# Two-layer decoder trunk: the four-expert round in fourth place, the rare-overflow branch and the overflow fetch behind round three, parameter rows behind the 37th expert unit

## The chip, the cores and the metric

The kernel runs on one NeuronCore of a Trainium2 chip. The metric is the device time of one execution in microseconds (us). The engines are named as in the profile: PE (TensorE, matrix multiplications; PEld is its weight load), DVE (VectorE), ACT (ScalarE), POOL (GpSimd) and SP (SyncE, which issues the transfers here); a q behind a name is the engine's sequencer, which runs branches, waits and the issue of transfers.

## The reference, cut to what matters

Two layers over 256 tokens of width 1024. Each layer is a token mixer (pooling, a gated convolution, differential attention and spatial gating, merged by gates) and then a mixture of experts; both end in a residual and a layer norm.

```python
def hierarchical_moe(x, w_rg, b_rg, w_re, b_re, w_gate, w_up, w_down):
    gl = (x @ w_rg + b_rg)                       # 4 groups
    pg = softmax(gl); g_sel = argmax(gl); p_sel = pg[g_sel]
    el = einsum('bsd,gde->bsge', x, w_re) + b_re # 4 experts in a group
    top_v, top_i = top_k(el[g_sel], 2)
    gate = softmax(top_v) * p_sel                # two experts of 16 per token
    ...
    for e in range(16):                          # width 1024 -> 256 -> 1024
        h = silu(x @ w_gate[e]) * (x @ w_up[e])
        out += gate[:, e] * (h @ w_down[e])
```

Which experts are full depends on the data. All weights have to come from memory once, since the on-chip memory holds a small part of them.

## The kernel before, in words

**Units and loads.** Weights arrive in units of 1 MB (class `Unit`, L117): one transfer each, issued by SP in the order in which the units are used. Fourteen buffers go round, so the load of unit i goes into the buffer of unit i-14 and is issued when that unit has been used. Units 0 to 47 of the expert part of a layer are three for each of 16 experts: two halves of gate and up (kh=0, kh=1) and one of down. Units 48 to 51 are the first four of the next layer, for the first layer alone.

**Rounds.** The experts run in seven rounds, p = 0 to 6, each with 128 gathered token slots. Rounds 0 to 2 take the first six experts in pairs of 64 slots. The other ten are sorted by their count of tokens: rounds 3 to 5 take the six fullest in pairs, round 6 the four emptiest at 32 slots each (`PAIRS`, `HALF`, `places`). The list `feed` gives the order of the units: for each round its gate and up units, then the down units of the round before. A four-expert round therefore has eight gate and up units and four down units, a pair four and two.

**Order of the work.** `pair(p)` writes it out by hand: `start(p+1)` (first halves of gate and up, L699), `turn(p)` (transposes on PE, L738 and L740, copied by ACT), the scatter of round p-1 into four accumulators (L715), `end(p+1)`, and `down(p)` (L707). I call the matmuls of L699 gu(round, half). `residual_mm` adds the residual in between. Behind round 5, `down7` is the second product of the last round, and its result goes through ACT and DVE (`y`, L96 and L97) into the last scatter, from which the layer norm starts. On ACT, the casts of the next layer's first units (`ahead`, L134) stand between.

**Branches.** An expert with more tokens than slots has an overflow. The usual case of one such chunk is handled in two blocks: the fetch of its three units (L797: ow twice, od; 3 MB), and its computation behind round 5 (L852). The fetch block is taken in the second layer and not in the first. Everything beyond that is in a third block, `rare` (L807), which holds further fetches and is not taken in either layer with this data. An engine that skips a block brings its semaphores to the state that they would have behind it. For SP this means eight semaphores of its transfers and one more.

**Parameter rows.** `lnp` (tile `gb2`, L815) are the scale and shift rows of the second layer norm, 1 MB. `rw` and `bc` (L1095, L1096) are small rows of the token mixer; those of the first layer are loaded at the start, those of the second during the first.

```python
        with tc.If(most > 16 * CAP + 15):          # L797
            fetch(0, ww, wd)
        ...
            si, todo = pair(NP - 4, si, todo)      # pair(3)
            residual_mm(0, hl)
            ps = start(NP - 2)                     # gu(5, 0)
        with tc.If(rest > 16 * CAP + 15, ...):     # L807
            steps.rare()
```

Of the kernel before, what the change touches and what calls it, by code (L numbers as in the profile page):

```python
# [11 lines left out]
F32 = mybir.dt.float32  # L12
# [21 lines left out]


STAT = 6
PAIRS = 6
HALF = CAP // 2
NP = PAIRS + 1
SLOTS = NP * 128  # L40
CYCLE = RAW + SPL
FIRST = CYCLE + 3
# [27 lines left out]
def trunk(ctx: ExitStack, tc: tile.TileContext, x, xT, wu, rows, brow, lnp, cst, ut, out):  # L70
# [40 lines left out]
    class Unit:  # L111


        def __init__(self, l, i, pieces=1, raw=None, src=None):
            self.raw = raw if raw is not None else raw_p.tile([P, 2048], F32, tag="raw", name=nm("raw"))
            if pieces:
                self.load = nc.sync.dma_start(self.raw, wu[l * NU + i] if src is None else src)  # L117
            self.parts = {}
            self.after = None

        def quarter(self, q):
            if q % 2 == 0:
# [294 lines left out]
    def tail(l, x_in, mhi, mlo, rw, wg, sw, unit, last):  # L417
# [15 lines left out]

        def places(p):

            w = CAP if p < PAIRS else HALF
            c, c0 = (0, p * P) if p < STAT // 2 else (1, (p - STAT // 2) * P)
            return [(2 * p + j, slice(j * w, (j + 1) * w), xg[c], slice(c0 + j * w, c0 + (j + 1) * w)) for j in range(P // w)]

        def places_n(p):  # L440
            return [2 * p + j for j in range(2 if p < PAIRS else 4)] if 0 <= p < NP else []

        feed = [f_ for p in range(NP + 1) for f_ in [(i, j) for j in range(2) for i in places_n(p)] + [(i, 2) for i in places_n(p - 1)]]
        at = {f_: i for i, f_ in enumerate(feed)}
# [104 lines left out]
        with manual():  # L549
# [66 lines left out]
                    gathered(0, k)  # L616

            key = sm.tile([P, 16], F32, tag="key", name=nm("key"))
            top = sm.tile([P, 20], F32, tag="top", name=nm("top"))
            topi = sm.tile([P, 20], I32, tag="topi", name=nm("topi"))  # L620
            ei = sm.tile([P, 20], I32, tag="ei", name=nm("ei"))

            def counts():

                V.scalar_tensor_tensor(key, cn, 16.0, down15, op0=OP.mult, op1=OP.add)
                V.max(top[:, 10:18], key[:, STAT:])
                low = sm.tile([P, 18], F32, tag="low", name=nm("low"))
                V.tensor_scalar(low[:, 0:10], key[:, STAT:], -1.0, None, op0=OP.mult)
                V.max(low[:, 10:18], low[:, 0:10])
                V.tensor_scalar(top[:, 16:20], low[:, 10:14], -1.0, None, op0=OP.mult)  # L630
                V.max(top[:, 0:8], key)
                V.scalar_tensor_tensor(top[:, 8:9], top[:, 0:1], -16.0 * MORE, top[:, 1:2], op0=OP.add, op1=OP.max)
                V.scalar_tensor_tensor(top[:, 8:9], top[:, 19:20], 16.0 * (CAP - HALF), top[:, 8:9], op0=OP.add, op1=OP.max)
# [16 lines left out]
            def slot_gates(p0, p1):  # L650
                gp = psumd()[:, :(p1 - p0) * 8].rearrange("p (a b) -> p a b", b=8)
                for p in range(p0, p1):
                    n = len(places_n(p))
                    for t in range(2):
                        T.matmul(gp[:, p - p0, :2 * n], Q[t][:, p * P:(p + 1) * P],
                                 rts[t].gh[:, 2 * p:2 * p + n, :].rearrange("p a b -> p (a b)"), start=(t == 0), stop=(t == 1))
                for a, b, n in ((p0, min(p1, PAIRS), 2), (max(p0, PAIRS), p1, 4)):
                    for j in range(n if a < b else 0):
                        r = slice(j * P // n, (j + 1) * P // n)
                        V.tensor_reduce(gs[r, a:b], gp[r, a - p0:b - p0, 2 * j:2 * j + 2], axis=AX.X, op=OP.add)  # L660

            def order():

                n = NE - STAT
                m = mp.tile([P, 2, n, 16], F32, tag="aT", bufs=2, name=nm("m"))
                V.tensor_tensor(m[:, 0], key[:, None, :].to_broadcast([P, n, 16]), top[:, 10:20, None].to_broadcast([P, n, 16]),
                                op=OP.is_equal)
                for t in range(2):
                    o = sm.tile([P, 2, n], F32, tag="ord", name=nm("ord"))
                    for i, v in enumerate((rts[t].s16, rts[t].g16)):  # L670
                        V.tensor_tensor(m[:, 1], m[:, 0], v[:, None, :].to_broadcast([P, n, 16]), op=OP.mult)
                        V.tensor_reduce(o[:, i], m[:, 1], axis=AX.X, op=OP.add)
                    slots(t, STAT * CAP, o[:, 0, :2 * PAIRS - STAT])
                    slots(t, 2 * PAIRS * CAP, o[:, 0, 2 * PAIRS - STAT:], HALF)
                    finish(rts[t].two(slice(STAT, NE), o[:, 1]))

            def spare(i, base, q, gt):
# [17 lines left out]
            def gu(p, kh, ps):  # L695
                w = [raw(i, kh) for i in places_n(p)]
                for k in range(4):
                    for (_, r, x_, c), w_ in zip(places(p), w):
                        T.matmul(ps[r, :], x_[:, 4 * kh + k, c], w_[:, k * 512:(k + 1) * 512],  # L699
                                 start=(kh == 0 and k == 0), stop=(kh == 1 and k == 3))  # L700

            def down(p, aT, pd, halves=(0, 1)):
                w = [raw(i, 2) for i in places_n(p)]
                for half in halves:
                    for k in range(2):
                        for (_, r, _, _), w_ in zip(places(p), w):
# [48 lines left out]

            ps = start(0)
            gu(0, 1, ps)
            slot_gates(0, STAT // 2)
            si = expert_act(ps, gs[:, 0:1])
            order()  # L760
            for t in range(2):
# [8 lines left out]
            def pair(p, si, todo, ps=None):  # L770
                ps = ps or start(p + 1)
                qt, aT = turn(p, si)
                if todo:
                    scatter(*todo)
                si = end(p + 1, ps)
                for k in more.get(p, ()):
                    for t in range(2):
                        gather(1, k, t)
                    gathered(1, k)
                if p == 1:  # L780
                    slot_gates(STAT // 2, NP)
# [4 lines left out]
            for p in range(1, NP - 4):  # L786
                si, todo = pair(p, si, todo)
                if p == 1:
                    most = nc.values_load(topi[0:1, 0:1], min_val=0, max_val=16 * S + 15)
# [1 line left out]
            oo = big.tile([P, 1040], F32, tag="tlo", name=nm("oo"))  # L791
            fq = [oo[:, 768 + t * P:768 + (t + 1) * P] for t in range(2)]
            fg = oo[:, 1024:1026]
            spare(0, CAP, fq, fg)
            ww = mp.tile([P, 4096], F32, tag="T16b", name=nm("ow"))
            wd = big.tile([P, 2048], F32, tag="thi", name=nm("od"))
        with tc.If(most > 16 * CAP + 15):  # L797
            fetch(0, ww, wd)
        steps = overflow(topi, (most, rest), spare, fetch, ww, wd, oo, fq, fg, x1, lambda: acc)
        with manual():  # L800
            hl = residual_parts(0)
            tc.mark_branch_hint_location(f"rare{l}", rest > 16 * CAP + 15, engines=(mybir.EngineType.PE,))
            si, todo = pair(NP - 4, si, todo)
            residual_mm(0, hl)
            ps = start(NP - 2)
        steps.room(big, "acc")
        with tc.If(rest > 16 * CAP + 15, label=f"rare{l}"):  # L807
            steps.rare()
        with manual():
            hl = residual_parts(1)  # L810
            si, todo = pair(NP - 3, si, todo, ps)
            tc.mark_branch_hint_location(f"past{l}", most > 16 * CAP + 15, engines=(mybir.EngineType.PE,))
            residual_mm(1, hl)
            gb2 = big.tile([P, 2, D], F32, tag="acc", name=nm("lnp"))
# [52 lines left out]
        with manual():  # L867
# [74 lines left out]
            else:  # L942
# [9 lines left out]
                for half in range(2):  # L952
                    done(1, half)
                nc.sync.dma_start(x2d, y)
        return None if last else (x2d, nhi, nlo, us[len(feed):])

    def overflow(topi, counts, spare, fetch, ww, wd, oo, q, gt, x1, sums):
# [96 lines left out]
        def fours(i):  # L1054

            k_ = nc.values_load(topi[0:1, i:i + 1], min_val=0, max_val=16 * S + 15)
            with tc.If(k_ > 16 * HALF + 15):
                with manual():
                    fetch(i, ww, wd)
                    chunk(i, HALF)  # L1060
                if i > 16:
                    fours(i - 1)

        def rare():

            past(counts[0], 0, CAP + MORE)
            experts(1)
            fours(19)
            with manual():
                spare(0, CAP, q, gt)  # L1070
                fetch(0, ww, wd)

        return SimpleNamespace(chunk=chunk, rare=rare, room=room)

    def layer(l, x_in, thi, tlo, last, early):
# [3 lines left out]
        def unit():  # L1079
# [3 lines left out]
                return early[i]  # L1083
            return Unit(l, i)

        lam_init = 0.8 - 0.6 * math.exp(-0.3 * l)
        tks = [slice(0, P), slice(P, 2 * P)]
        merged = big.tile([P, 2, D], F32, tag="acc", name=nm("acc"))
# [2 lines left out]
        us = [unit() for _ in range(2)]  # L1091
        rw = big.tile([P, W_N], F32, tag="rw", name=nm("rw"))
        bc = big.tile([P, B_N], F32, tag="bc", name=nm("bc"))
        with tc.issue_after(early[2].load.ins) if l == 0 else nullcontext():
            nc.sync.dma_start(rw, rows[l])  # L1095
            nc.sync.dma_start(bc, brow[l].partition_broadcast(P))  # L1096

# [384 lines left out]
```

## Time and profile before

| what | value |
|---|---|
| median of three runs | 687.53 us (686.36 to 689.56) |
| the profiled execution's own time | 687.56 us |
| its span, first to last instruction | 685.8 us |
| mean granted TensorE clock | 0.986 |
| PE busy | 652.8 us, 95% of the span |
| DVE, ACT busy | 60%, 42% |

PE is busy in nearly all of the span, so that the time is PE's work plus the stretches in which PE waits. A row of the waits names who waited, at which line, on what, the total, the number of times and the longest. A granted clock of 1.00 is the upper of TensorE's two levels, 2.4 GHz, and 0.50 the lower, 1.2 GHz. The expert part of the second layer stands 335.1 us behind that of the first.

### The profile page before, as it was taken

The page shows a single profiled execution, that of the slowest core. Times are in us where ns is not written, and L with a number is a line of the kernel's source. Part 1 is how long each engine was busy: PE and PEld are TensorE (multiplying, and loading weights), DVE is VectorE, ACT ScalarE, POOL GpSimd, SP SyncE. Part 2 cuts the span into 40 slices and gives each one's busy share as a digit, 9 for nine tenths or more (in the row PEclk, how much of TensorE's full clock was granted, in tenths as well). Part 3 has the DMA queues.
Part 4 walks back from the last instruction along what each step waited for, and adds up shares of the span by engine and source line. Part 5 has one row for each costly group of instructions (what it writes and reads, how often), then busy time and mean ns, then how long its engine had stood idle before and what let it go on. Part 6 is the DMA issues. An engine that isn't in the chain of part 4 may idle for free. (4 is left out here: it accounts for less than half of the span.)

```text
span 685.8 us, 9776 instructions
## 1 busy us (share of the span) xinstructions
PE 652.8 (95%) x3579; PEld 462.3 (67%) x3579; DVE 412.3 (60%) x932; ACT 287.0 (42%) x465; POOL 5.9 (1%) x26
## 2 busy tenths in 40 slices
PE   8999999999999999998699999999999999999983
PEld 5899778888888354333479987888887953543331
DVE  4998667876557832211799875786853677321116
ACT  5755675454224231111455547664441252211122
POOL 0100000000000000000000000000000000000000
PEclk9999999999999999999899999999999999999997
DMA  8995544466759997979927363456566799699871
GB/s 302 369 338 190 206 131 176 172 219 224 289 192 391 410 419 290 396 291 424 421 100 275 123 236 105 152 183 249 182 225 265 271 409 421 261 402 418 318 326 62
DMA packets 28001, 185.73 MB, mean 271 GB/s; under 512 B 3104, under 2 KB 3232, under 8 KB 6432
## 3 DMA queue, kind: packets, MB, share of 16 engines
q1 hardware_dynamic: 27936, 184.94, 70.4%
q8 instruction: 32, 0.52, 0.3%
q14 instruction: 33, 0.27, 0.1%
HBM read 182.83 MB, written 2.10 MB: 270 GB/s over the span
## 5 line engine op out<-in xcount | busy, mean ns | idle before, releaser
L138 DVE TENSOR_TENSOR sp<-raw,sp 128x1024 fp32r<-128x1024 f32 x122 | 147.9, 1221 | 53.7 <-ACT sp L134 43.6
L134 ACT CAST sp<-raw 128x1024 fp32r<-128x1024 f32 x122 | 126.0, 1051 | 105.3 <-PE mm L229 72.5
L229 PE MATMUL mm<-sp,thi 128*128 128x512 f32 (+1 forms) x320 | 96.5, 382 | 1.5 <-ACT sp L96 0.9
L229 PE MATMUL mm<-sp,nhi 128*128 128x512 f32 (+1 forms) x320 | 97.4, 382 | 0.3 <-ACT nhi L96 0.3
L699 PE MATMUL ps<-wr,xg 128*64 128x512 f32 (+1 forms) x352 | 80.0, 596 | 0.0
L229 PEld LDWEIGHTS mm<-sp,thi 128*128 128x128 f32 x320 | 58.9, 188 | 13.5 <-ACT sp L96 1.5
L229 PEld LDWEIGHTS mm<-sp,nhi 128*128 128x128 f32 x320 | 58.8, 188 | 11.7 <-issue 0.5
L229 PE MATMUL mm<-sp,nlo 128*128 128x512 f32 (+1 forms) x160 | 61.4, 385 | 0.5 <-DVE nlo L97 0.4
L229 PE MATMUL mm<-sp,tlo 128*128 128x512 f32 (+1 forms) x160 | 60.1, 380 | 0.0
L699 PEld LDWEIGHTS ps<-wr,xg 128*64 128x64 f32 (+1 forms) x352 | 23.0, 128 | 37.2 <-issue 36.5
L229 PE MATMUL dn<-sp,yhl 128*128 128x512 f32 x192 | 47.8, 392 | 0.0
L409 DVE SCALAR_TENSOR_TENSOR si<-ps,gs,si 128x256 f32<-128x256 f32 x14 | 6.8, 483 | 62.6 <-ACT si L408 62.4
L699 PE MATMUL ps<-raw,xg 128*64 128x512 f32 (+1 forms) x144 | 43.2, 596 | 0.8 <-DVE xg L541 0.8
L229 PE MATMUL mm<-sp,mhl 128*128 128x512 f32 (+1 forms) x192 | 41.0, 368 | 0.9 <-ACT mhl L96 0.5
L229 PEld LDWEIGHTS dn<-sp,yhl 128*128 128x128 f32 x192 | 35.8, 188 | 7.4
L229 PEld LDWEIGHTS mm<-sp,mhl 128*128 128x128 f32 x192 | 32.6, 189 | 7.5 <-DVE mhl L97 1.1
L229 PE MATMUL mm<-thi,sp 128*128 128x256 f32 x192 | 35.6, 286 | 1.4 <-ACT scr L1225 1.3
L229 PE MATMUL mm<-nhi,sp 128*128 128x256 f32 x192 | 35.7, 286 | 0.3 <-ACT misc L1122 0.3
L97 DVE TENSOR_TENSOR yy<-dn,yy 128x512 fp32r<-128x512 f32 x24 | 16.4, 690 | 31.8 <-ACT yy L96 31.8
L229 PEld LDWEIGHTS mm<-sp,nlo 128*128 128x128 f32 x160 | 30.1, 188 | 6.6 <-DVE nlo L97 1.0
L229 PEld LDWEIGHTS mm<-sp,tlo 128*128 128x128 f32 x160 | 30.1, 188 | 5.5
L707 PE MATMUL dn<-wr,aT 128*64 128x512 f32 x112 | 31.5, 613 | 2.2 <-DMA wr<-in_wu_dram 2.2
(305 smaller groups left out, 974.8 us busy)
## 6 DMA issues: line engine op xcount, KB each, us to landing
raw<-in_wu_dram SPq DMA_DIRECT2D x91, 1024.0 KB, 5.2
wr<-in_wu_dram SPq DMA_DIRECT2D x63, 1024.0 KB, 9.5
w<-in_wu_dram SPq DMA_DIRECT2D x6, 1024.0 KB, 14.9
raw<-in_wu_dram SPq DMA_DIRECT2D x8, 256.0 KB, 6.0
lnp<-in_lnp_dram SPq DMA_DIRECT2D x4, 512.0 KB, 6.0
lnp<-in_lnp_dram SPq DMA_DIRECT2D x2, 1024.0 KB, 15.7
ow<-in_wu_dram SPq DMA_DIRECT2D x2, 1024.0 KB, 10.6
xr<-in_xT_dram SPq DMA_DIRECT2D x4, 256.0 KB, 5.8
```

What stands on the lines that cost most here:

```text
L97: eng.tensor_tensor(lo, src, f32(hi), op=OP.subtract)
L134: A.copy(self.parts[q][0], self.raw[:, q * 1024:(q + 1) * 1024])
L138: V.tensor_tensor(lo, self.raw[:, q * 1024:(q + 1) * 1024], f32(hi), op=OP.subtract)
L229: T.matmul(ps, a, b, start=(first and i == 0), stop=(last and i == n - 1))
L409: V.scalar_tensor_tensor(si, ps[:, 256:512], gate, si, op0=OP.mult, op1=OP.mult)
L699: T.matmul(ps[r, :], x_[:, 4 * kh + k, c], w_[:, k * 512:(k + 1) * 512], start=(kh == 0 and k == 0), stop=(kh == 1 and k == 3))
L707: T.matmul(pd[half][r, :], aT[:, k, r], w_[:, k * 1024 + half * 512:k * 1024 + (half + 1) * 512], start=(k == 0), stop=(k == 1))
```

## The change

The four-expert round moves from place 6 to place 3 (`FOUR`), so the order of the expert units changes from the 17th on. The branch of the rare overflow moves forward by one round, and the fetch branch moves behind it. The rows `rw` and `bc` of the second layer are tied to the load of the first layer's 37th unit (`us[36]`); in SP's order both stand between the loads of units 37 and 38, counted from zero. Before, `rw` stood between the loads of units 27 and 28, and `bc` was loaded in the mixer of the first layer.

```diff
+FOUR = STAT // 2
-NP = PAIRS + 1
+NP = 7
...
         def places(p):
-            w = CAP if p < PAIRS else HALF
+            w = HALF if p == FOUR else CAP
...
         def places_n(p):
-            return [2 * p + j for j in range(2 if p < PAIRS else 4)] if 0 <= p < NP else []
+            a = 2 * p + 2 * (p > FOUR)
+            return list(range(a, a + (4 if p == FOUR else 2))) if 0 <= p < NP else []
...
-            spare(0, CAP, fq, fg)
             ww = mp.tile([P, 4096], F32, tag="T16b", name=nm("ow"))
             wd = big.tile([P, 2048], F32, tag="thi", name=nm("od"))
-        with tc.If(most > 16 * CAP + 15):
-            fetch(0, ww, wd)
         steps = overflow(topi, (most, rest), spare, fetch, ww, wd, oo, fq, fg, x1, lambda: acc)
-        with manual():
-            hl = residual_parts(0)
-            tc.mark_branch_hint_location(f"rare{l}", rest > 16 * CAP + 15, engines=(mybir.EngineType.PE,))
-            si, todo = pair(NP - 4, si, todo)
-            residual_mm(0, hl)
-            ps = start(NP - 2)
         steps.room(big, "acc")
         with tc.If(rest > 16 * CAP + 15, label=f"rare{l}"):
             steps.rare()
         with manual():
+            spare(0, CAP, fq, fg)
+        with tc.If(most > 16 * CAP + 15):
+            fetch(0, ww, wd)
+        with manual():
+            hl = residual_parts(0)
+            si, todo = pair(NP - 4, si, todo)
+            residual_mm(0, hl)
             hl = residual_parts(1)
-            si, todo = pair(NP - 3, si, todo, ps)
+            si, todo = pair(NP - 3, si, todo)
...
+            us[-1].before = us[36]
...
-        with tc.issue_after(early[2].load.ins) if l == 0 else nullcontext():
+        with tc.issue_after(turn_of(early).load.ins):
             nc.sync.dma_start(rw, rows[l])
             nc.sync.dma_start(bc, brow[l].partition_broadcast(P))
```

On SP, the first layer's rare branch stood behind the load of unit 42 (the last `wr` here); the fetch branch L797 stood eight loads further up, behind unit 34:

```order
L117 ISA
L117 DMA wr_2872<-in_wu_dram 128x2048
L117 ISA
L117 DMA wr_2903<-in_wu_dram 128x2048
L117 ISA
L117 DMA wr_2915<-in_wu_dram 128x2048
L807 COMPARE_AND_BRANCH
L1038 COMPARE_AND_BRANCH x5
```

Now it stands behind the load of unit 38, the last `wr` here, with `rw` and `bc` between 37 and 38 (L800 is the line of the rare branch in the changed file, L1098 and L1099 those of `rw` and `bc`):

```order
L117 ISA
L117 DMA wr_2738<-in_wu_dram 128x2048
L1098 DMA rw_6740<-in_rows_dram 128x956
L1099 DMA bc_6741<-in_brow_dram 128x916
L117 ISA
L117 DMA wr_2750<-in_wu_dram 128x2048
L800 COMPARE_AND_BRANCH
```

The fetch branch (L804) now follows at the end of the rare block, and the load of unit 39 comes behind the fetch's three transfers:

```order
L1058 UNCONDITIONAL_BRANCH x5
L800 UNCONDITIONAL_BRANCH
L804 COMPARE_AND_BRANCH
L641 TENSOR_LOAD ei_2115
L641 ISA x2
L693 ISA
L693 DMA ow_2777<-in_wu_dram 128x2048
```

So the same eight-semaphore skip, the three fetches, and `rw` and `bc` stand ahead of unit 39, where before the skip stood ahead of unit 43 and the fetches ahead of unit 35.

At the end of the first layer's list, SP issued unit 47 (raw_6388), then `lnp`, then units 48 to 51:

```order
L117 DMA raw_6388<-in_wu_dram 128x2048
L815 DMA lnp_6375<-in_lnp_dram 128x2048
L117 DMA raw_6390<-in_wu_dram 128x2048
L117 DMA wr_6392<-in_wu_dram 128x2048
L117 DMA wr_6394<-in_wu_dram 128x2048
L117 DMA wr_6429<-in_wu_dram 128x2048
```

and now it issues 47 (raw_6329) and 48 to 51 first, and `lnp` behind them:

```order
L117 DMA raw_6329<-in_wu_dram 128x2048
L117 DMA raw_6331<-in_wu_dram 128x2048
L117 DMA wr_6358<-in_wu_dram 128x2048
L117 DMA wr_6360<-in_wu_dram 128x2048
L117 DMA wr_6375<-in_wu_dram 128x2048
L815 DMA lnp_6398<-in_lnp_dram 128x2048
```

`lnp` is thus five transfers later among the same loads.

On PE, gu(5, 0) and the transposes of turn(4) stood ahead of the rare branch, and the scatter behind it:

```order
L699 MATMUL ps_2902<-wr_2585,xg_2452 64x512
L699 MATMUL ps_2902<-wr_2530,xg_2452 64x512
L699 MATMUL ps_2902<-wr_2585,xg_2452 64x512
L738 MATMUL ps_6276<-cs,Q_1776 128x128
L738 MATMUL ps_6276<-cs,Q_1777 128x128
L740 MATMUL ps_6276<-cs,si_2855 128x128 x2
L807 COMPARE_AND_BRANCH
```

now it is gu(4, 0) and the transposes of turn(3):

```order
L699 MATMUL ps_6154<-wr_2518,xg_2452 64x512
L699 MATMUL ps_6154<-wr_2429,xg_2452 64x512
L699 MATMUL ps_6154<-wr_2518,xg_2452 64x512
L738 MATMUL ps_6187<-cs,Q_1776 128x128
L738 MATMUL ps_6187<-cs,Q_1777 128x128
L740 MATMUL ps_6187<-cs,si_2733 128x128 x2
L800 COMPARE_AND_BRANCH
```

So PE meets the branch one round earlier, with the same kind of work queued ahead of it.

The units that the rounds use, by number, are these. Before: gu(5) 28 to 31, down(4) 32 and 33, gu(6) 34 to 41, down(5) 42 and 43, `down7` 44 to 47. After: gu(3) 16 to 23, down(2) 24 and 25, gu(4) 26 to 29, down(3) 30 to 33, gu(5) 34 to 37, down(4) 38 and 39, gu(6) 40 to 43, down(5) 44 and 45, `down7` 46 and 47.

## Rows read from the trace of the kernel before

**Rows 1.** The page's first lines: busy us, share of the span, instructions.

```profile
span 685.8 us, 9776 instructions
...
PE 652.8 (95%) x3579; PEld 462.3 (67%) x3579; DVE 412.3 (60%) x932; ACT 287.0 (42%) x465; POOL 5.9 (1%) x26
```

**Rows 2.** Timeline of PE: start, us, work, idle time before it and its releaser.

```profile
322.77 0.62 PE L707 MATMUL ps<-raw,aT 128*32 128x512 f32 x1 [1.34 <-DMA raw<-in_wu_dram]
...
331.86 0.79 PE L715 MATMUL mm<-y,QT 128*128 128x512 f32 x1 [5.47 <-ACT y L96]
...
653.08 0.65 PE L707 MATMUL dn<-wr,aT 128*64 128x512 f32 x2 [2.19 <-DMA wr<-in_wu_dram]
```

**Rows 3.** Waits of SP around the rare branch, first and second layer: total, times, longest.

```profile
SPq L807 <- SPq L807: 12.3, 3, 5.6
...
SPq L807 <- SPq L807: 18.9, 7, 5.1
```

**Rows 4.** Line 807, the rare branch: instructions, ns, first and last start.

```profile
L807 SPq EVENT_SEMAPHORE  x9: 17/17/17, 633.9 to 647.8; - x9
...
L807 ACTq EVENT_SEMAPHORE  x2: 17/17/17, 293.7 to 293.8; - x2
...
L807 ACTq COMPARE_BRANCH  x1: 45/45/45, 288.6 to 288.6; - x1
```

**Rows 5.** Timeline of SP's issues: units 28, 34, 35, 42, 49; then 42, 43 of layer two.

```profile
262.80 0.33 SPq L117 DMA_DIRECT2D wr<-in_wu_dram  x1
...
275.68 0.33 SPq L117 DMA_DIRECT2D raw<-in_wu_dram  x1
276.81 0.34 SPq L117 DMA_DIRECT2D wr<-in_wu_dram  x1
...
293.27 0.33 SPq L117 DMA_DIRECT2D wr<-in_wu_dram  x1
...
310.55 0.48 SPq L117 DMA_DIRECT2D wr<-in_wu_dram  x1
...
628.38 0.33 SPq L117 DMA_DIRECT2D wr<-in_wu_dram  x1
...
648.13 0.34 SPq L117 DMA_DIRECT2D wr<-in_wu_dram  x1
```

**Rows 6.** Issue to landing, us: units 28, 42, 49; then 42 of layer two.

```profile
wr<-in_wu_dram SPq DMA_DIRECT2D x1, 1024.0 KB, 4.9
...
wr<-in_wu_dram SPq DMA_DIRECT2D x1, 1024.0 KB, 12.7
...
wr<-in_wu_dram SPq DMA_DIRECT2D x1, 1024.0 KB, 19.6
...
wr<-in_wu_dram SPq DMA_DIRECT2D x1, 1024.0 KB, 19.3
```

**Rows 7.** Stretches by window: us, busy by engine, granted clock, DMA share, GB/s.

```profile
653.62:657.04 3.42, 3.25 (x8) 0.62 (x4) 0.09 (x1) 0.59 (x1) 0.00 (x0) 0.50 1.02 434
...
331.90:336.00 4.10, 3.52 (x8) 2.46 (x9) 3.59 (x7) 2.28 (x3) 0.00 (x0) 0.50 1.03 430
```

**Rows 8.** Timeline of PE: down(4) in both layers.

```profile
299.63 0.60 PE L707 MATMUL dn<-raw,aT 128*64 128x512 f32 x2
...
634.72 0.60 PE L707 MATMUL dn<-raw,aT 128*64 128x512 f32 x2
```

**Rows 9.** Issue to landing of the mixer's rows, over the span: count, KB, us.

```profile
rw<-in_rows_dram SPq DMA_DIRECT2D x2, 478.0 KB, 5.6
...
bc<-in_brow_dram SPq DMA_DIRECT2D x2, 458.0 KB, 7.1
```

**Rows 10.** Timeline of ACT and DVE at the first layer's end.

```profile
330.28 1.04 ACT L134 CAST sp<-wr 128x1024 fp32r<-128x1024 f32 x1 [0.52 <-DMA wr<-in_wu_dram]
...
336.67 0.75 DVE L295 SCALAR_TENSOR_TENSOR y<-mm,nmv,lnp 128x512 f32<-128x512 f32 x1
```

**Rows 11.** Waits of PE over the span, at line 715.

```profile
PE mm L715 <- PEq L807: 0.6, 2, 0.3
```

More of the change, by code (lines that the diff above doesn't have):

```diff
@@ L36 @@
 STAT = 6
-PAIRS = 6
+FOUR = STAT // 2
 HALF = CAP // 2
-NP = PAIRS + 1
+NP = 7
 SLOTS = NP * 128
@@ L118, in __init__ @@
             self.parts = {}
-            self.after = None
+            self.after = self.before = None
         def quarter(self, q):
@@ L434, in places @@
         def places(p):
-            w = CAP if p < PAIRS else HALF
-            c, c0 = (0, p * P) if p < STAT // 2 else (1, (p - STAT // 2) * P)
-            return [(2 * p + j, slice(j * w, (j + 1) * w), xg[c], slice(c0 + j * w, c0 + (j + 1) * w)) for j in range(P // w)]
+            w = HALF if p == FOUR else CAP
+            c, c0 = (0, p * P) if p < FOUR else (1, (p - FOUR) * P)
+            return [(slice(j * w, (j + 1) * w), xg[c], slice(c0 + j * w, c0 + (j + 1) * w)) for j in range(P // w)]
         def places_n(p):
-            return [2 * p + j for j in range(2 if p < PAIRS else 4)] if 0 <= p < NP else []
+            a = 2 * p + 2 * (p > FOUR)
+            return list(range(a, a + (4 if p == FOUR else 2))) if 0 <= p < NP else []
         feed = [f_ for p in range(NP + 1) for f_ in [(i, j) for j in range(2) for i in places_n(p)] + [(i, 2) for i in places_n(p - 1)]]
@@ L618, in tail @@
             key = sm.tile([P, 16], F32, tag="key", name=nm("key"))
-            top = sm.tile([P, 20], F32, tag="top", name=nm("top"))
-            topi = sm.tile([P, 20], I32, tag="topi", name=nm("topi"))
-            ei = sm.tile([P, 20], I32, tag="ei", name=nm("ei"))
+            top = sm.tile([P, 22], F32, tag="top", name=nm("top"))
+            topi = sm.tile([P, 22], I32, tag="topi", name=nm("topi"))
+            ei = sm.tile([P, 22], I32, tag="ei", name=nm("ei"))
             def counts():
                 V.scalar_tensor_tensor(key, cn, 16.0, down15, op0=OP.mult, op1=OP.add)
-                V.max(top[:, 10:18], key[:, STAT:])
+                V.max(top[:, 14:22], key[:, STAT:])
                 low = sm.tile([P, 18], F32, tag="low", name=nm("low"))
@@ L629, in counts @@
                 V.max(low[:, 10:18], low[:, 0:10])
-                V.tensor_scalar(top[:, 16:20], low[:, 10:14], -1.0, None, op0=OP.mult)
+                V.tensor_scalar(top[:, 10:14], low[:, 10:14], -1.0, None, op0=OP.mult)
                 V.max(top[:, 0:8], key)
                 V.scalar_tensor_tensor(top[:, 8:9], top[:, 0:1], -16.0 * MORE, top[:, 1:2], op0=OP.add, op1=OP.max)
-                V.scalar_tensor_tensor(top[:, 8:9], top[:, 19:20], 16.0 * (CAP - HALF), top[:, 8:9], op0=OP.add, op1=OP.max)
+                V.scalar_tensor_tensor(top[:, 8:9], top[:, 13:14], 16.0 * (CAP - HALF), top[:, 8:9], op0=OP.add, op1=OP.max)
                 V.tensor_copy(top[:, 9:10], top[:, 8:9])
@@ L652, in slot_gates @@
                 for p in range(p0, p1):
-                    n = len(places_n(p))
+                    e = places_n(p)
                     for t in range(2):
[L655 to L659, printed above, removed]
+                        T.matmul(gp[:, p - p0, :2 * len(e)], Q[t][:, p * P:(p + 1) * P],
+                                 rts[t].gh[:, e[0]:e[-1] + 1, :].rearrange("p a b -> p (a b)"), start=(t == 0), stop=(t == 1))
+                for a, b in ((0, FOUR), (FOUR, FOUR + 1), (FOUR + 1, NP)):
+                    for j, (r, _, _) in enumerate(places(a) if p0 <= a < p1 else ()):
                         V.tensor_reduce(gs[r, a:b], gp[r, a - p0:b - p0, 2 * j:2 * j + 2], axis=AX.X, op=OP.add)
@@ L672, in order @@
                         V.tensor_reduce(o[:, i], m[:, 1], axis=AX.X, op=OP.add)
-                    slots(t, STAT * CAP, o[:, 0, :2 * PAIRS - STAT])
-                    slots(t, 2 * PAIRS * CAP, o[:, 0, 2 * PAIRS - STAT:], HALF)
+                    slots(t, FOUR * P, o[:, 0, :4], HALF)
+                    slots(t, (FOUR + 1) * P, o[:, 0, 4:])
                     finish(rts[t].two(slice(STAT, NE), o[:, 1]))
@@ L697, in gu @@
                 for k in range(4):
-                    for (_, r, x_, c), w_ in zip(places(p), w):
+                    for (r, x_, c), w_ in zip(places(p), w):
                         T.matmul(ps[r, :], x_[:, 4 * kh + k, c], w_[:, k * 512:(k + 1) * 512],
@@ L705, in down @@
                     for k in range(2):
-                        for (_, r, _, _), w_ in zip(places(p), w):
+                        for (r, _, _), w_ in zip(places(p), w):
                             T.matmul(pd[half][r, :], aT[:, k, r], w_[:, k * 1024 + half * 512:k * 1024 + (half + 1) * 512],
@@ L757, in tail @@
             gu(0, 1, ps)
-            slot_gates(0, STAT // 2)
+            slot_gates(0, FOUR)
             si = expert_act(ps, gs[:, 0:1])
@@ L780, in pair @@
                 if p == 1:
-                    slot_gates(STAT // 2, NP)
+                    slot_gates(FOUR, NP)
                 return si, out_(p, qt, aT)
@@ L786, in tail @@
             for p in range(1, NP - 4):
+                if p == NP - 5:
+                    tc.mark_branch_hint_location(f"rare{l}", rest > 16 * CAP + 15, engines=(mybir.EngineType.PE,))
                 si, todo = pair(p, si, todo)
@@ L1060, in fours @@
                     chunk(i, HALF)
-                if i > 16:
+                if i > 10:
                     fours(i - 1)
         def rare():
+            fetch(0, ww, wd)
             past(counts[0], 0, CAP + MORE)
             experts(1)
[L1068 to L1071, printed above, removed]
+            fours(13)
         return SimpleNamespace(chunk=chunk, rare=rare, room=room)
@@ L1084, in unit, with turn_of @@
             return Unit(l, i)
+        def turn_of(early):
+            return early[-1].before or early[-1]
         lam_init = 0.8 - 0.6 * math.exp(-0.3 * l)
```

## The prediction, made before the changed kernel ran

> **What bounds the kernel now.** I read the page first: PE is busy for 652.8 of 685.8 us [rows 1]. PE's work is the same after the change (the same experts, the same slots, the same matmuls in another order), so only PE's waits and the stretches at the lower clock can move the time. The second view is PE's own timeline at its longer waits [rows 2]. Three of them belong to the expert part: 1.34 us for a raw unit and 5.47 us at the end of the first layer, and 2.19 us for a wr unit late in the second. Two of these releasers are transfers, and the third, ACT's `y`, turns out to be one too (below). So the kernel is bound by PE, and near the end of both layers by the loads.
>
> The third view is SP around the rare branch. SP waits 12.3 us there in the first layer and 18.9 us in the second [rows 3]. The longest piece, 5.6 and 5.1 us, is the jump. The rest is nine semaphore instructions that end at 647.8 us in the second layer [rows 4]. Unit 42 was issued at 628.38 and took 19.3 us, so it landed at 647.7 [rows 5, 6]. The next load left at 648.13 [rows 5]. Skipping the block therefore holds SP until every load in flight has landed: the transfers run empty once per layer. The Trainium skill, page "DMA: Bandwidth & Descriptors", section "Anatomy of one DMA — SWDGE (gpsimd) path", says that DMA engines never wait on semaphores and that the issuing sequencer does it before dispatch. The trace agrees, with SP's 18.9 us, and by that rule moving the branch can move the hole but not close it.
>
> What is a hole worth? A lone load takes 4.9 us from issue to landing (unit 28 [rows 5, 6]). In an undisturbed stretch the transfers carry 430 GB/s [rows 7], which is 1.049 MB / 430 = 2.44 us for a unit. From unit 28 (landed 262.80 + 4.9 = 267.7) to unit 42 (293.27 + 12.7 = 306.0) the first layer brought 14 loads, 2.73 us each [rows 5, 6]. The second layer is 634.72 - 299.63 = 335.1 us behind [rows 8], so its unit 28 lands at 602.8; from there to 647.7 it brought 14 units and three fetches, 17 loads at 2.64 us. I take 2.64 for the sum, with 2.44 and 2.73 as the bounds. Unit 28 waits for its buffer, that is for PE's down(1), in both versions, so these two landings stay where they are.
>
> **What the change does, part by part.** *The branch and the fetch.* Now the hole stands behind unit 38 instead of 42, and down(4) is the first to need 39. Down(4) starts at 299.63 and 634.72 us before [rows 8]. I keep these as the times of need, as the rounds ahead of it are one four-expert round and pairs in place of pairs alone, with the same slots.
>
> Second layer: unit 38 lands at 602.8 + 10 x 2.64 = 629.2. SP needs 0.4 us for its semaphores (647.7 to 648.13) and 1.1 us for the fetch branch, which I price by the skip of L797 (275.68 to 276.81, both [rows 5]); below nothing is excluded, since it stands in line on SP, and taking it instead of skipping it may cost a little more. Then the first fetch lands 4.9 us later, at 635.6, and ahead of 39 stand three fetches, so 39 lands at 635.6 + 3 x 2.64 = 643.5. PE waits from 634.72: **8.8 us** (6.2 at 2.44, 10.1 at 2.73).
>
> A wait of 2.19 us was followed by 3.42 us at a granted clock of 0.50, the lower level of 1.2 GHz, which loses 1.7; one of 5.47 us by 4.1 us at 0.50, which loses 2.05 [rows 2, 7]. I add 2.05 for this wait. The old wait of 2.19 and its 1.7 go: unit 43, which it waited for, lands at 643.5 + 4 x 2.64 = 654.1, as late as before, but PE is now ten microseconds further behind. Second layer: 8.8 + 2.05 - 2.19 - 1.7 = **+7.0**.
>
> The Trainium skill gives, on the same page and in the same section, a fixed cost of about 2 us for a transfer. The row of 4.9 us less 2.44 gives 2.5, and by the page's 2.0 (an estimate from that page) the stall would be 8.3 instead of 8.8.
>
> First layer: there is no fetch, but `rw` and `bc` are ahead of the hole, 478 + 458 KB [rows 9], at the same rate 2.4 us. They were loaded elsewhere before, where PE shows no wait for them; I put their removal there at nothing (if they had delayed a load there, it would gain at most these 2.4). Unit 38 lands at 267.7 + 26.4 + 2.4 = 296.5, and 39 at 296.5 + 1.5 + 4.9 = 302.9, against 299.63: a wait of 3.3 (1.1 to 4.4), with 1.7 for the clock, less the 1.34 that goes. This would be +3.7 in the middle of the layer.
>
> *The end of the first layer* decides what of it stays. Unit 49 was issued at 310.55 and took 19.6 us, so it landed at 330.15 [rows 5, 6]; ACT's cast of it began at 330.28, held by that transfer [rows 10]. In ACT's order `y` comes behind this cast, and PE's last scatter waits for `y` until 331.86, 5.47 us [rows 2]. So it is a wait for a load. After, PE would have finished `down7` at 331.86 - 5.47 + 3.7 = 330.1, and 49 lands at 302.9 + 10 x 2.64 = 329.3, earlier than before because `lnp` no longer stands ahead of it. With the same 1.7 from landing to scatter (330.15 to 331.86), PE goes on at 331.0, and the wait is short enough that perhaps no half clock follows. That alone would be a gain of 1 to 3 us.
>
> But `lnp` now stands behind 51, the 13th load behind 39: it lands at 302.9 + 13 x 2.64 = 337.2. DVE multiplies by it at L295, at 336.67 before [rows 10], and the next layer's first matmuls hang on that norm. So L295 moves to 337.3: first layer **+0.6**. At 2.44 (39 at 300.7) `lnp` lands at 332.4, and L295 could start 4.3 earlier; at 2.73 (39 at 304.0) it lands at 339.5 and costs 2.9. Whatever is lost on PE inside this layer is swallowed by that wait.
>
> *The jump on the other engines.* ACT's took 293.7 - 288.6 = 5.1 us [rows 4], and PE lost only 0.3 us of it per layer [rows 11], since a gu and a turn were queued ahead. The same kind of work stands ahead now, so I put it at nothing. Without that cover it costs up to 5.1 per layer, but PE then comes later to the same late load and the stall shrinks by as much. The Trainium skill, page "Runtime: NRT & Kernel Launch", section "Instruction fetch mechanics", says that a branch to a target outside the fetched window has to fetch it first. The trace agrees with 5.1 us; no term changes by it. `spare` and the other moved DVE work run while PE waits.
>
> **Sum.** 687.56 + 7.0 + 0.6 = 695.2 us by the profiled execution, which stands 0.03 above the median of the runs shown (687.53). Forecast 695.1.
>
> **The rivals.** *A, the forecast*: the hole meets a buffer that is too short, 695.1. *B, stalls only trade places*: the loads run at 2.44 throughout. Then the second layer is 6.2 + 1.7 - 3.9 = +4.0 and the first -4.3: 687.3 to 691. For it speaks that the stretches at the end do run so [rows 7]; against it, that over 14 and 17 loads neither layer did. *C, faster*: the hole does not reach PE. For that, 39 must land by 634.72, so 38 by 634.72 - 14.3 = 620.4, ten loads in 17.6 us, 1.76 each. No row shows that rate; it could happen only if SP did not wait for all the loads at the new place, so that nothing runs empty. Then the second layer gains 3.9 and the first the 4.3: 679.4. *D, slower still*: at 2.73 the second layer is 10.1 + 2.05 - 3.9 = +8.3 and the first +2.9, which gives 698.8; units 41 and 45 late as well would add a microsecond or two.
>
> **Chances.** A 0.60, B 0.20, C 0.08, D 0.12. A measurement of this kernel tells a change of about 0.5% (3.4 us) from none. Faster by more than that is C: 0.08. Within 0.5% (684.1 to 691.0) is nearly all of B and the lowest edge of A: 0.22. Slower: 0.70. The range runs from the low end of B, 687.3, to a little above D, 699.5, which leaves out C and the far end of D. The likeliest case's own range is 691.5 to 698.
>
> **What would show it.** In the trace after: a PE wait at L707 on a wr transfer near 635 us of about 9 us, with the clock at 0.50 behind it; one of some 3 us near 300; none at down(5) in the second layer. SP's next transfer behind the rare branch at about 297 and 630 instead of 306 and 648. L295 of the first layer released by `lnp` and not by DVE's own work. Wrong would be: unit 38 landing far ahead of 629 (then the rate is mis-sized), the first transfer behind the branch leaving before 38 has landed (then there is no drain, C), or PE reaching down(4) much later than 634.72, so that its round order costs PE time of its own and the stall is smaller than it looks.

## The result, and the profile after

The changed kernel takes 695.81 us (median of four runs, 694.78 to 697.81) against 687.2 for the kernel before, run beside it; the ratio is 1.0123, with a 95% interval of 1.0086 to 1.016. The forecast was 695.1, slower. The profiled execution took 694.79 us; the two longest of the four (696.8 and 697.8) have a mean granted clock of 0.982, the other two 0.987 and 0.990.

The page's first lines of the changed kernel answer to [rows 1]. The span grew by 7.2 us. PE's busy time grew by 3.6 although its 3579 instructions are the same; part of that is work at the lower clock.

```profile
span 693.0 us, 9786 instructions
...
PE 656.4 (95%) x3579; PEld 463.9 (67%) x3579; DVE 412.7 (60%) x932; ACT 287.3 (41%) x465; POOL 6.0 (1%) x26
```

PE's timeline at down(4) of both layers answers to [rows 8] and [rows 2]. The columns are start, us, work, and the idle time ahead of it.

```profile
300.84 1.02 PE L707 MATMUL dn<-wr,aT 128*64 128x512 f32 x2
303.78 0.65 PE L707 MATMUL dn<-wr,aT 128*64 128x512 f32 x2 [1.92 <-DMA wr<-in_wu_dram]
...
635.89 1.02 PE L707 MATMUL dn<-wr,aT 128*64 128x512 f32 x2
644.26 5.55 PE L707 MATMUL dn<-wr,aT 128*64 128x512 f32 x14 [7.36 <-DMA wr<-in_wu_dram]
```

In both layers two matmuls of unit 38 run and PE then waits for unit 39. The waits at down(5) of the second layer and at the raw unit in the first, which stand in [rows 2], are gone (0.7 us remains near 320).

SP's issues in the second layer answer to [rows 5]: unit 38, the first of the overflow's fetches, and unit 39.

```profile
611.34 0.33 SPq L117 DMA_DIRECT2D wr<-in_wu_dram  x1
...
630.87 1.66 SPq L693 DMA_DIRECT2D ow<-in_wu_dram  x2
...
634.54 0.33 SPq L117 DMA_DIRECT2D wr<-in_wu_dram  x1
```

Their times from issue to landing, in the same order (the third is unit 39):

```profile
wr<-in_wu_dram SPq DMA_DIRECT2D x1, 1024.0 KB, 18.2
...
ow<-in_wu_dram SPq DMA_DIRECT2D x1, 1024.0 KB, 4.8
...
wr<-in_wu_dram SPq DMA_DIRECT2D x1, 1024.0 KB, 9.7
```

So unit 38 landed at 629.5, SP issued nothing until 630.87, the first fetch landed at 635.7 and unit 39 at 644.2. SP's own wait at the rare branch (now L800) in the second layer, and the semaphores of that branch, answer to [rows 3, 4]; the last of nine passes at 629.6, a tenth behind unit 38's landing.

```profile
SPq L800 <- SPq L800: 17.6, 6, 5.3
...
L800 SPq EVENT_SEMAPHORE  x9: 17/17/17, 617.1 to 629.6; - x9
```

Two windows behind the waits (us, busy by engine, clock, DMA share, GB/s) answer to [rows 7]. Behind the second layer's wait the granted clock is 0.50, behind the first layer's it stays at 1.00.

```profile
644.20:648.00 3.80, 3.74 (x10) 1.25 (x12) 0.00 (x0) 0.03 (x1) 0.00 (x0) 0.50 1.01 429
...
303.80:308.00 4.20, 4.20 (x17) 1.58 (x18) 0.69 (x1) 1.12 (x2) 0.21 (x2) 1.00 1.00 423
```

And the end of the first layer, where DVE now waits for `lnp` (compare [rows 10]):

```profile
337.45 0.75 DVE L295 SCALAR_TENSOR_TENSOR y<-mm,nmv,lnp 128x512 f32<-128x512 f32 x1 [1.48 <-DMA lnp<-in_lnp_dram]
```

To see in which layer a version gains or loses, I cut each profiled span at the first gather matmul of each layer (L533 in the kernel before, L534 in the changed one). The middle piece holds the first layer's experts and the second layer's mixer, the last piece the second layer's experts.

| us | before that | first layer's experts | second layer's experts | span |
|---|---|---|---|---|
| before | 212.6 | 335.1 | 138.2 | 685.8 |
| after | 213.0 | 335.0 | 145.1 | 693.0 |

All of the loss, 6.9 us, is in the second layer.

### The profile page after: what moved, and what is told of

Read it like the earlier page. It is cut to its first block, busy times and chain, and to the rows that moved or that the text cites. A ratio compares the mean times of both kernels' runs of the same rounds, so it can differ in the third digit from the quotient of the medians.

```text
span 693.0 us, 9786 instructions
## 1 busy us (share of the span) xinstructions
PE 656.4 (95%) x3579; PEld 463.9 (67%) x3579; DVE 412.7 (60%) x932; ACT 287.3 (41%) x465; POOL 6.0 (1%) x26
## 5 line engine op out<-in xcount | busy, mean ns | idle before, releaser
L699 PE MATMUL ps<-wr,xg 128*64 128x512 f32 (+1 forms) x352 | 87.8, 597 | 0.0
L229 PEld LDWEIGHTS mm<-sp,thi 128*128 128x128 f32 x320 | 58.8, 188 | 14.3 <-ACT sp L96 1.6
L699 PEld LDWEIGHTS ps<-wr,xg 128*64 128x64 f32 (+1 forms) x352 | 26.7, 132 | 36.2 <-issue 33.9
L707 PE MATMUL dn<-wr,aT 128*64 128x512 f32 (+1 forms) x128 | 40.8, 631 | 9.3 <-DMA wr<-in_wu_dram 9.3
L699 PE MATMUL ps<-raw,xg 128*64 128x512 f32 (+1 forms) x144 | 36.0, 596 | 0.8 <-DVE xg L542 0.8
L96 ACT CAST yy<-dn 128x512 fp32r<-128x512 f32 x24 | 14.1, 587 | 49.6 <-PE dn L707 44.7
```

The costliest lines, as they stand in the source:

```text
L96: A.copy(hi, src)
L229: T.matmul(ps, a, b, start=(first and i == 0), stop=(last and i == n - 1))
```

## The experiments

Five theories were tested. 1: the hole that SP's skip leaves, and the three fetches behind it, make unit 39 late. 2: the new order of the rounds costs by itself. 3: the jump costs, not the wait for transfers. 4: moving the rare branch forward costs by itself. 5: `rw` and `bc` ahead of the branch are a main cause. (A sixth concerns `lnp`. What the run "the kernel before, with the rare block's fetches on GpSimd" calls theory 3 is another one: that the hole by itself is worth nothing.) Ratios are to the kernel before, run beside each version on the same chip.

**The rare block left out.**

```diff
-        with tc.If(rest > 16 * CAP + 15, label=f"rare{l}"):
-            steps.rare()
```

> The changed kernel without the block of the rare overflow, which is not taken with this data (so it leaves out the handling of more than one overflow chunk). Theory 1 (the hole): with nothing to skip, SP doesn't run empty. Unit 38 lands at about 629.5 us as in the changed kernel, the three fetches and unit 39 follow 2.48 us apart, so 39 lands near 639.5 and the stall of 7.4 us at down(4) of the second layer shrinks to about 4; in the first layer the stall of 1.9 us goes and the lnp rows land some 3 us earlier, at 334.4. Time 689 us (687 to 691). Theory 2 (the order of the rounds itself eats the units faster than they come): both stalls stay, 694 to 697 us.

Measured 682.78 us, 0.990 (0.988 to 0.993). PE's wait for a wr unit in the second layer is halved, and the first layer has none:

```profile
PE dn L707 <- DMA wr<-in_wu_dram: 3.4, 1, 3.4
```

Theory 1's stall (about 4) came out, and theory 2 falls as the sole cause. The time is 6 us below my number. Of that the first layer gave 3: 39 landed at 299.4 and `lnp` at 331.7, not at the 334.4 that I had added up, and that layer's piece is 329.4 against 335.0. The profiled execution is the longest of its five (685.64), so its pieces do not show the rest.

**The rare block kept, its fetches on GpSimd.**

```diff
 def fetch(i, ww, wd, pool=False):
-    nc.sync.dma_start(w, unit_of(i, j))
+    if pool: nc.gpsimd.dma_start(w, unit_of(i, j, mybir.EngineType.Pool))
+    else: nc.sync.dma_start(w, unit_of(i, j))
 ...
 # in the rare block:
-    fetch(i, ww, wd)
+    fetch(i, ww, wd, True)
```

> The changed kernel with the fetches inside the rare block issued by GpSimd instead of SP; the block still stands there and is skipped. Theory 1: what holds SP is the semaphores of its own transfers that the block would use. GpSimd's are idle, so nothing waits, and the time is that without the block plus the jump (0.7 us on PE per layer): 690 us (688 to 692), the first transfer behind the branch leaving before 38 has landed. Theory 3 (the jump itself, 5 us on each engine, is what costs): no change, 694 to 697 us.

Measured 685.12 us, 0.995 (0.993 to 0.997), some 5 us below my number: the two layers' pieces, 331.5 and 138.8, are 3.5 and 6.3 shorter than in the changed kernel, and I had counted 5.8 in all. SP still jumps. Its issues of unit 38, of the fetches and of unit 39, and unit 38's landing time:

```profile
606.68 0.33 SPq L117 DMA_DIRECT2D wr<-in_wu_dram  x1
610.90 1.68 SPq L696 DMA_DIRECT2D ow<-in_wu_dram  x2
...
615.23 0.33 SPq L117 DMA_DIRECT2D wr<-in_wu_dram  x1
...
wr<-in_wu_dram SPq DMA_DIRECT2D x1, 1024.0 KB, 18.4
```

The first fetch leaves at 610.9, while unit 38 lands at 625.1. So what empties the transfers is the wait for SP's own transfers, not the jump: theory 3 falls. The remaining stall is 2.8 us:

```profile
PE dn L710 <- DMA wr<-in_wu_dram: 2.8, 1, 2.8
```

**The fetch branch behind the load of unit 46.**

```diff
-        with tc.If(most > 16 * CAP + 15):
-            fetch(0, ww, wd)
         with manual():
             hl = residual_parts(0)
             si, todo = pair(NP - 4, si, todo)
             residual_mm(0, hl)
+        with tc.If(most > 16 * CAP + 15):
+            fetch(0, ww, wd)
+        with manual():
             hl = residual_parts(1)
```

> The changed kernel with the fetch branch behind pair(3) and the residual, so that the three fetches come behind units 39 to 46 and not ahead of them. Theory 1: the hole stays, but 39 is the first load behind it and lands at 630.9 + 4.9 = 635.8 us, just as down(4) needs it: the stall of 7.4 us in the second layer and the 1.9 us at the lower clock behind it go. First layer as it is, or 1 us less since one branch leaves the path. Time 686 us (685 to 688). Theory 2 (order of the rounds): 694 to 697 us.

Measured 683.94 us, 0.993 (0.991 to 0.996), 2 us below my number, though the pieces (334.1 and 135.8) are 0.9 and 9.3 shorter, about as I had counted. The hole is still there: unit 39 left at 627.94, behind unit 38's landing at 627.6. PE nevertheless waits in the second layer for no wr unit at all, only 0.3 us for a fetch that now comes late:

```profile
PE dn L1009 <- DMA ow<-in_wu_dram: 0.3, 1, 0.3
```

So hole and fetches are not two separate prices. In the second layer either one alone is mostly covered by the units that lie ready (2.8 us of stall without the hole, none without the fetches), and together they are not.

**The kernel before, with the rare block's fetches on GpSimd** (the same edit as above).

> The kernel before with the fetches inside the rare block issued by GpSimd. Theory 1: the hole of the kernel before goes too. Second layer: the 2.19 us at down(5) and the 1.7 us at the lower clock go. First layer: unit 49 lands 3 us earlier, so the last scatter starts at about 329 instead of 331.9. Time 680 us (678 to 682). Theory 3 (the hole is worth nothing by itself, only its place against the need): within 1 us of the kernel before.

Measured 679.97 us, 0.988 (0.985 to 0.990), as theory 1 says. The stall of 2.19 us is gone, and the wait at the first layer's end is shorter than the 5.47 of [rows 2]; unit 49 landed at 326.3 instead of 330.2:

```profile
PE mm L718 <- ACT y L96: 3.7, 1, 3.7
```

**The order of the rounds alone**: the four-expert round in fourth place, and both branches, `rw` and `bc` as in the kernel before.

```diff
 # after, with the branches put back:
+        with tc.If(most > 16 * CAP + 15):
+            fetch(0, ww, wd)
...
             si, todo = pair(NP - 4, si, todo)
             residual_mm(0, hl)
+            ps = start(NP - 2)
+        with tc.If(rest > 16 * CAP + 15, label=f"rare{l}"):
+            steps.rare()
```

> The four-expert round in fourth place alone: both branches stand where they stand in the kernel before (fetch behind round 2, rare behind round 4's first halves), rw and bc where they stood. Theory 1: the order of the rounds costs only that unit 39 is needed at down(4) and now comes behind the three fetches: in the second layer a stall of about 4 us and 1.9 us at the lower clock. The hole comes behind unit 47 and reaches no need in the second layer, so the 2.19 us and 1.7 us of before go; first layer 4 us shorter, since units 48 and 49 land earlier. Time 685 us (683 to 688). Theory 2 (the order itself is what made the changed kernel slower): 694 to 697 us.

Measured 684.32 us, 0.994 (0.992 to 0.997). So the new order is no loss, and theory 2 falls. The gain lies in the first layer alone (its piece is 329.6 against 335.1, the second's 139.7 against 138.2). Unit 49 lands there at 324.6 instead of 330.2, with `lnp` now behind it, and the clock at that layer's end stays at 1.00; what of the gain is the order, what `lnp`'s place and what the clock was not separated. The second layer has a stall of 3.0 us behind the fetches, and no lower clock follows it:

```profile
PE dn L707 <- DMA wr<-in_wu_dram: 3.0, 1, 3.0
...
635.00:639.00 4.00, 3.93 (x16) 1.36 (x17) 0.69 (x1) 0.83 (x2) 0.00 (x0) 1.00 1.00 416
```

**The rare branch alone moved one round forward, in the kernel before.**

```diff
         with tc.If(most > 16 * CAP + 15):
             fetch(0, ww, wd)
+        with tc.If(rest > 16 * CAP + 15, label=f"rare{l}"):
+            steps.rare()
         ...
             residual_mm(0, hl)
-            ps = start(NP - 2)
-        with tc.If(rest > 16 * CAP + 15, label=f"rare{l}"):
-            steps.rare()
```

> The kernel before with the rare branch alone moved one round forward, right behind the fetch branch; order of rounds, fetch, rw and bc as before. Theory 1: the hole now follows unit 34 and the fetches, and unit 35 lands near 290 and 631.5 us, while gu(6) needs units 35 to 37 at 304 and 639. So the hole meets a buffer that is long enough: the stall of 2.19 us at down(5) of the second layer shrinks to about 1 and the first layer's end comes 3 us earlier. Time 682 us (680 to 686). Theory 4 (moving the rare branch forward costs by itself, through its jump or since more is in flight there): 690 us or more.

Measured 687.94 us, 1.000 (0.997 to 1.002): neither theory's number. The first layer's piece gained 1.9 us (333.2), but the second's did not (138.5). PE's timeline at the second halves of gate and up of round 6 shows why: the stall of 2.19 us did not shrink, it moved to unit 41.

```profile
645.31 2.04 PE L699 MATMUL ps<-wr,xg 128*32 128x512 f32 x6
648.79 3.19 PE L699 MATMUL ps<-wr,xg 128*32 128x512 f32 x25 [1.43 <-DMA wr<-in_wu_dram]
```

These matmuls end at 652.0 instead of 649.0 in the kernel before, 3.0 us later, of which the trace names 1.43 as a wait. From the 631.5 that I had put for unit 35, unit 41 would have come at 646.4 (six loads, 2.48 apart); it landed at 648.7, since unit 35 came at 632.4 and not 631.5, and one step of the stream took 3.8 us (642.5 to 646.3) instead of 2.5. Theory 4's 690 or more was not reached: moving the hole forward neither pays nor costs here.

**Both causes taken away**: the fetch behind unit 46 and the rare fetches on GpSimd (the two edits above together).

> The changed kernel with the fetch branch behind pair(3) and the residual, and the rare block's fetches issued by GpSimd: both causes gone. Theory 1: no stall at down(4) in either layer, none later; against the run with GpSimd's fetches alone the 2.84 us and 1.9 us of the second layer go: 680 us (678.5 to 682), level with the kernel before that has GpSimd's fetches. If the order of rounds has a price of its own, it stays above that one by it.

Measured 680.05 us, 0.988 (0.984 to 0.991), with no wait for a unit in either layer. It stands level with the kernel before that has the GpSimd edit, so the order of rounds has no price left; with `rw` and `bc` in their old place too, as in the next run, the new order is 3.6 us ahead of that kernel (676.41 against 679.97).

**The same, with `rw` and `bc` loaded as in the kernel before.**

```diff
-        with tc.issue_after(turn_of(early).load.ins):
+        with tc.issue_after(early[2].load.ins) if l == 0 else nullcontext():
             nc.sync.dma_start(rw, rows[l])
             nc.sync.dma_start(bc, brow[l].partition_broadcast(P))
```

> As late_pool, with rw and bc of the second layer where the kernel before loads them. Theory 1: the first layer's loads from unit 38 on land 2.4 us earlier; unit 49 and lnp do too, of which the end of the first layer (where ACT's casts of 48 and 49 stand ahead of y) gives back up to 2 us: 678.5 us (677 to 680.5). If PE and not the loads sets the end of the first layer there, no difference from late_pool.

Measured 676.41 us, 0.983 (0.980 to 0.986): faster than both kernels. The first layer's piece is 327.9 against late_pool's 330.9, so the rows cost 3.0 there and not the 1.5 that I had counted; the range that I gave went down to 677 only. Its page begins:

```profile
span 675.2 us, 9807 instructions
...
PE 649.3 (96%) x3579; PEld 459.8 (68%) x3579; DVE 411.9 (61%) x932; ACT 287.2 (43%) x465; POOL 5.9 (1%) x26
```

**`rw` and `bc` back in the changed kernel** (the edit above alone).

> The changed kernel with rw and bc of the second layer where the kernel before loads them, so 0.94 MB less ahead of the hole in the first layer; the second layer's expert part is untouched. Theory 1: units 38, 39 and lnp land 2.4 us earlier in the first layer; the 1.9 us wait at down(4) there goes, and L295, which waited 1.5 us for lnp, starts some 2.4 us earlier, at 335.0. The stall of 7.4 us in the second layer stays as it is. Time 693.4 us (692 to 695). Theory 5 (rw and bc ahead of the branch are a main cause of the loss): 690 us or less, or a smaller stall in the second layer.

Measured 692.18 us, 1.007 (1.004 to 1.009). The first layer's piece fell to 331.9 (3.1 us less), the second's stayed at 145.7, with the stall where it was:

```profile
PE dn L707 <- DMA wr<-in_wu_dram: 8.0, 1, 8.0
```

So theory 5 falls as a main cause: these rows cost some 3 us in the first layer and nothing in the second.

**`lnp` between units 49 and 50 in the changed kernel.**

```diff
-            nc.sync.dma_start(gb2, lnp[l, 2:4].partition_broadcast(P))
+            gbl.append(nc.sync.dma_start(gb2, lnp[l, 2:4].partition_broadcast(P)))
 # units 50 and 51 are issued after it:
+                    with tc.issue_after(gbl[0].ins) if gbl else nullcontext():
```

> The changed kernel with lnp issued between units 49 and 50 instead of behind 51; nothing else moves. Theory 1 (in the first layer's end lnp is what lands last): lnp lands at about 332.5 instead of 337.4 us, L295 no longer waits for it and starts 1.5 us earlier, near 336.0, and the next layer's first transposes at 339.1 instead of 340.5. Time 694.3 us, too little for the time alone; the profile decides. Theory 6 (lnp is only the last named of several and PE's scatter sets the end): L295 and the transposes stay within 0.5 us of where they are.

Measured 692.87 us, 1.007 (1.004 to 1.010); I had said that the time is too near to tell. In the profile L295 follows the instruction ahead of it without a wait, and the next layer's transposes come earlier:

```profile
335.11 0.74 DVE L295 SCALAR_TENSOR_TENSOR y<-mm,nmv,lnp 128x512 f32<-128x512 f32 x1
...
338.25 0.38 PE L256 MATMUL ps<-cs,y 128*128 128x128 f32 x2
```

The first layer's piece is 333.3, 1.7 us less than in the changed kernel (1.5 expected). So `lnp` was the last to land there, and theory 6 falls.

**The fastest version with the same edit.**

> The fastest version so far (new order of rounds, fetch behind pair(3), rare fetches on GpSimd, rw and bc as before) with the same edit. L295 waited 0.9 us for lnp there; that goes: 675.5 us (674 to 677).

Measured 676.51 us, 0.983 (0.979 to 0.987): the first layer's piece gained another 1.1 us (326.8), DVE waits for nothing there any more, and the time is that of the version without it within its spread. In the profile the second layer's piece is 1.7 us longer (135.9 against 134.2); the last section shows why.

## Why the prediction was right, point by point

**The drain.** Right, and shown: SP's next transfer left at 630.87 (630.7 forecast), and with nothing of its own to wait for (the run with the fetches on GpSimd) it left while unit 38 was still 14 us from landing.

**Unit 39 of the second layer.** Forecast 643.5, landed 644.2. The rate of 2.64 held on the whole: ten units from 28 to 38 took 26.5 us (603.0 to 629.5), and the three fetches and unit 39 another 14.7 (14.3 forecast).

**The stall.** Forecast 8.8, measured 7.36. The term was too large because of the time of need: PE reached down(4) at 635.9 and not 634.7, and did two matmuls of unit 38 before it needed 39. Of the 1.2 us, 0.3 were there at the start of the layer's experts and 0.4 is the jump (0.73 us at L800 against 0.30 in [rows 11]), which I had put at nothing; I did not settle the rest. But the sum does not feel this. PE goes on when unit 39 lands, and what PE lost earlier only shortens the wait. Second layer: +7.0 forecast, +6.9 measured. That it fits to 0.1 is luck: unit 39 came 0.7 later than forecast, the two matmuls that PE had already done took about 0.5 off the work behind it, and the clock cost 0.15 less. (The forecast's upper bound for this wait adds up to 10.0 and not 10.1; nothing hangs on it.)

**The clock.** 3.8 us at 0.50 cost 1.9 (2.05 forecast). The size was right. Whether it comes at all is less certain than the forecast had it: behind the first layer's wait it put a stretch at the lower clock too, and there was none (see the last section).

**The first layer.** In its middle I forecast a wait of 3.3 and 1.7 at the lower clock; it was 1.92, since PE came 1.2 us later there too and did two matmuls first; the clock stayed at 1.00, which nothing here explains. The short wait at the layer's end, behind which I thought that perhaps no lower clock would follow, was followed by one (0.50 from 335 to 337), without effect, since L295 waited for `lnp` until after that. At its end `lnp` landed at 337.43 (337.2 forecast), and L295 started at 337.45 (337.3). The layer's net was forecast at +0.6 and measured at -0.1; L295 came 0.4 later when counted from the start of that layer's experts, and I did not trace where the next mixer won this back. That `lnp` sets it is shown by the run that moved it; that the rows `rw` and `bc` stand behind some 3 us of it (2.4 forecast), by the run that put them back.

**The sum.** By the profiled executions the change is 7.2 us (7.6 forecast), by the medians 8.6. The 1.4 between the two is not accounted for by any term above; executions of the changed kernel alone differ by 3.0.

**What the prediction did not say.** It took the hole and the fetches as one sum. The experiments show how they combine: by the medians (the kernel before, run beside each version, stood between 687.2 and 688.3) the changed kernel is 10.7 us faster without the hole, 11.9 without the fetches ahead of unit 39, and 15.8, not their sum, without both. By the pieces the second layer is 6.3, 9.3 and 9.3 shorter. The last of these profiles has 3.4 us at the lower clock late in that layer (650.8 to 654.2), and the other two have none, so with the fetches further back the hole is still worth up to 1.7 there. In the first layer its removal brings 3.2 (330.9 against 334.1). And the kernel with the new order of the rounds, which I had held to be neutral, is faster by about half a per cent where the branches stay put.

## What to carry to other kernels

A branch that is never taken can hold a queue: look at what an engine must wait for when it skips the block, and where that engine has transfers in flight, let another engine, one that has none in flight, issue the block's transfers. Count a late load from its landing, with everything that stands ahead of it in the queue; what compute loses before that point does not add to the sum. And when loads are reordered, look for the last of them that the next stage needs, small parameter rows included, because the end of the stage follows that one.

## What the runs showed of the hardware that was not expected

The lower clock did not follow the length of the wait. A wait of 2.19 us was followed by 3.4 us at 0.50 in the kernel before [rows 2, 7], one of 3.0 us in the run with the new order alone by 4 us at 1.00. In the run without the rare block a wait of 3.4 us was followed by 1.00 for a good microsecond and then by 0.50; the row is the mean of both:

```profile
633.60:637.40 3.80, 3.76 (x12) 1.20 (x13) 0.62 (x1) 0.59 (x1) 0.00 (x0) 0.67 1.03 429
```

Behind the three longest waits of all runs (7.4, 7.6 and 8.0 us, at the same place in the changed kernel and two versions of it) the clock is 0.50 each time.

The clearest pair is the fastest version with and without `lnp` moved. Both run the same matmuls in the second layer and have the same wait of 1.09 us there. Behind it the first has 3.4 us at 0.50 and the second 3.4 us at 1.00, which is the 1.7 us between their second layers:

```profile
645.49 0.44 PE L1001 MATMUL dn<-cs,oo 128*128 128x128 f32 x2 [1.09 <-DVE yy L97]
646.80:650.20 3.40, 3.40 (x20) 1.01 (x20) 0.00 (x0) 0.40 (x1) 0.00 (x0) 0.50 1.00 414
...
647.14 0.44 PE L998 MATMUL dn<-cs,oo 128*128 128x128 f32 x2 [1.09 <-DVE yy L97]
648.45:651.85 3.40, 3.40 (x73) 2.04 (x69) 0.69 (x1) 0.58 (x1) 0.00 (x0) 1.00 1.01 419
```

The runs don't settle what decides it. A difference of 1 to 2 us between two profiles can therefore be the clock alone.

Loads of 1 MB mostly land 2.48 us apart, but now and then one lands 3 to 4 us behind the load ahead of it. In the changed kernel the second load behind the second layer's hole has such a step (635.7 to 639.3), and the transfers carried less in it. But the step does not belong to the hole: the run with the new order alone has one in a full stream (626.6 to 630.0), in which the transfers moved nearly as fast as ever, and none in the five loads behind its hole in the first layer.

```profile
635.68:639.25 3.57, 1.23 (x4) 0.14 (x1) 0.48 (x1) 0.38 (x1) 0.00 (x0) 1.00 0.97 365
...
626.56:630.04 3.48, 3.48 (x17) 1.47 (x17) 1.23 (x1) 0.55 (x3) 0.00 (x0) 1.00 1.02 414
```

The last two columns are the share of the DMA engines and GB/s. Where the step comes from is open. What I took as an average rate of 2.64 us is 2.48 and these steps.
